# Neighbourhood attention: the block exchange done once per pair of heads

## The chip, the cores and the metric

One Trainium2 chip; the kernel runs on one of its cores. The metric is device time in microseconds (us). The engines are TensorE (PE in the profile, its weight loads PEld), VectorE (DVE), ScalarE (ACT), GpSimd (POOL) and the sync engine (SP), which here only issues DMA transfers. Each engine works through its own queue in order.

## What is computed

One step of a two-layer trunk: 512 latent tokens on an 8 x 64 grid and 128 prompt tokens, 1024 wide, 16 heads of 64. Layer 0 mixes tokens by 2-D neighbourhood attention, layer 1 by grouped-query attention; a gated ConvFFN follows each. The change touches only the attention of layer 0:

```python
s_lat = einsum('brqhd,brkwhd->bhrqkw', qg, kg) * scale        # latent keys: 8 rows x 64 columns
s_lat = where(col_ok, s_lat + bias, -inf)                      # 16 columns around the query's
s_ctx = einsum('brqhd,bchd->bhrqc', qg, k_ctx) * scale         # 128 cached context keys
p = softmax(concatenate([s_lat, s_ctx]))
o = p_lat @ v_lat + p_ctx @ v_ctx                              # then o @ w_o: the output projection
```

Everything is float32. The large products are made of three products of a high and a low part each (`passes`, `wsplit`).

## The kernel before

**One head.** `Head(h)` has four score tiles (slots 0 to 3, 128 queries each). `scores(slot)` issues two products on TensorE into a PSUM bank, the addition of the bias table and the minimum on VectorE, the exponential on ScalarE, a reciprocal on VectorE, the scaling on GpSimd and a transpose on VectorE, which works within blocks of 32 x 32. What it leaves in `p` must still be moved between the partitions, 32 at a time: `exchange` does that with 16 transfers on the sync queue from `p` to `px`. The transfer for target group k and source group q takes 32 partitions and reads all four slots, so the first of them must wait for the last slot.

**A pair of heads.** `values(two)` multiplies the exchanged blocks of an even head and the odd one behind it with the value tiles, 24 products into one bank (`po`), reading `px` through `block`. ScalarE then copies the result to an output tile `of` (one for each pair, 128 x 640). Pairs 0 to 3 are stored to DRAM (`of_store`) and read back later (`ofr`), pairs 4 to 7 stay. `o_split(p)` makes the high and low parts `oh` and `ol` that the output projection reads; `m0.part0(t, p)` is one part of that projection, three products of 512 columns for token tile t and pair p (`y` in the profile).

**The order of the work.** A helper binds all instructions of TensorE to the order in which they are written. The other engines' instructions are ordered by the framework's scheduler at build time, those that it finds ready first, mostly in the order of the program. The loop over the heads follows lists of steps. While head h is in the loop, `s0` to `s3` are the score tiles of head h + 1, `x` its exchange, `f` one part of other TensorE work (`fill`), `a` a part of the modulation row (`ada`), `p0` to `p2` prompt attention (only where h % 4 is 1), `v` the values of heads h - 1 and h. `ORDER0` is for h = 0, `ORDER[0]` for even and `ORDER[1]` for odd heads below 13, `ORDER2` for those from 13 on. A last `f` of a list is left out where h % 4 is 0 and h > 0.

Up to head 12 the work behind `f` is the projection to queries, keys and values (`qk`, `vp`: 6 or 9 products), 173 parts in all, and then four parts of the output projection. What is left after head 12 is worked off, and 26 further parts of the output projection (pairs 2 to 5 for two token tiles, pairs 0 to 5 for the other three) are then spread by `f` over the last heads. Behind the loop stand part 6 for all five token tiles, the split of output tile 7, and part 7.

**Buffers.** `p` and `px` have two buffers of one head (6 KB per partition each), `of` four, the bias table `tb` two, the raw weights `wr` four slots. All weight loads stand in the same sync queue as the exchange and the stores.

Of the kernel before, what the change touches and what calls it, by code (L numbers as in the profile page):

```python
# [10 lines left out]
F32 = mybir.dt.float32  # L11
# [8 lines left out]
P = 128  # L20
# [5 lines left out]
NT = T // P  # L26
# [11 lines left out]
GAP = T + 2  # L38
QW = T + 64
NPT = 2  # L40
NPX = 2
NOF = 4
QD = 32
NAR = 2
OW = {0: 0, 2: 1, 4: 2}
# [3 lines left out]
NC = 3  # L49
QKH = (slice(0, 256), slice(256, T))  # L50
CTX = 2
ORDER0 = "f s0 f f s1 f f s2 f f a f s3 f f f x f f f".split()
ORDER = (
    "f s0 f f s1 f f s2 f f a f s3 f f f x f f f".split(),
    "p0 f s0 f f s1 f p1 f f s2 f f v a p2 s3 f f x".split(),
)
ORDER2 = (
    "f s0 f f s1 f f s2 f f f s3 f f f x f f f".split(),
    "p0 f s0 f f s1 f p1 f f s2 f f v p2 s3 f f x".split(),
)  # L60
PRO = 20
PSTEP = (4, 6, 6, 7, 8, 9)
# [12 lines left out]
def raw_ap(ap, offset, dims):  # L75
    return bass.AP(tensor=ap.tensor, offset=ap.offset + offset, ap=[list(d) for d in dims])
# [30 lines left out]
def hybrid_step(ctx: ExitStack, tc: tile.TileContext, A, O):  # L107
    nc = tc.nc
# [9 lines left out]
    def mm(*a, **k):  # L118
        pe(nc.tensor.matmul(*a, **k))  # L119

    def turn(*a, **k):
        pe(nc.tensor.transpose(*a, **k))  # L122
# [7 lines left out]
    def pool(name, bufs=1, side="left", **k):  # L130
        return tc.tile_pool(name=name, bufs=bufs, side=side, reuse_waits="tile", **k)

    cst = ctx.enter_context(pool("cst"))
    wp = ctx.enter_context(pool("wp", 4))
# [79 lines left out]
    class Halves:  # L214
# [5 lines left out]
        def __init__(self, keep, tmp):  # L220
            self.B = {n: [keep.tile([P, 4, TH], F32R, name=f"B{n}{i}") for i in range(2)] for n in ("11", "21")}
            self.h = tmp.tile([P, KC, 2 * TH], F32, name="hF")
            for c0, c1 in ((NS, NS + 1), (GAP - 1, 2 * TH)):
                nc.gpsimd.memset(self.h[:, :, c0:c1], 0.0)

        def block(self, i, j, c0=0, c1=TH):
            return self.h[:, 4 * i : 4 * i + 4, TH * j + c0 : TH * j + c1]
# [106 lines left out]
    def drain(gen):  # L334
        for _ in gen:
            pass
# [140 lines left out]
    def of_tile(p):  # L477

        if p not in of0:
            of0[p] = opool.tile([P, T], F32, tag="of", name=f"of{p}", bufs=NOF)  # L480
        return of0[p]
# [229 lines left out]
    def prompt_turn(ap, pp, tag, nb):  # L711
        tp = bk.get("tp")
        for i in range(4):
            turn(tp[:, i * P : i * P + P], pp[:, i, :], ident)
        x = ap.tile([P, 512], F32, tag=tag, name="ptp", bufs=nb)
        nc.scalar.copy(x, tp)
        bk.put(tp)
        return x.rearrange("p (a b) -> p a b", a=4)
# [68 lines left out]
    with l_na:  # L787
        ap = l_na.enter_context(pool("na", 2))
# [144 lines left out]
        def na_table(h):  # L933
            if h not in runs:
                na_runs(h)
            tr = runs.pop(h)
            tb = tbs[h % 2]
            for w, dst in ((1, tb[:, 0::6, :]), (0, tb[:, 1:3, :]), (0, tb[:, 4:6, :])):
                t0 = tr[:, w, :]
                rv = raw_ap(t0, RUN - 1, [t0.ap[0], [-16, 2], [-1, 16], [-31, 8]])  # L940
                i = nc.gpsimd.tensor_sub(
                    dst.rearrange("p c (a b) -> p c a b", b=8),
                    mask[:, w].rearrange("p (c a) b -> p c a b", c=2), rv,
                )
                if h == 2:
                    behind(i, plast[0])
            return tb

        class Head:


# [5 lines left out]

            def __init__(self, h):
                self.h, self.b = h, h % 2
                self.p4 = ap.tile([P, 4, 4, 3, QD], F32, tag="p", name="p", bufs=NPT)  # L960
                self.tb = na_table(h)
                self.nm = sm.tile([P, 4], F32, name="nm")
                self.su = sm.tile([P, 4], F32, name="su")
                self.rc = sm.tile([P, 4], F32, name="rc")
# [23 lines left out]

            def exchange(self):

                self.px = ap.tile([P, 4, 4, 3, QD], F32, tag="px", name="px", bufs=NPX)
                for q in range(4):
                    for k in range(4):
                        nc.sync.dma_start(self.px[QD * k : QD * k + QD, q], self.p4[QD * q : QD * q + QD, k])

            def block(self, s0, s1):

                c0 = 3 * QD * s0[0] + QD * s0[1]
                c1 = 3 * QD * s1[0] + QD * s1[1]
                return raw_ap(self.px, c0, [self.px.ap[0], [c1 - c0, 2], [12 * QD, 4], [1, QD]])  # L1000

        def values(two):

# [17 lines left out]
        m0 = Mix(0, A["na_w_o"][0], lambda p, t: tuple(x[:, t * P : t * P + P] for x in osp0[p]))  # L1021
# [44 lines left out]
        work = stream()  # L1066
# [5 lines left out]
        def fill(n=1):  # L1072
            for _ in range(n):
                next(work, None)
# [3 lines left out]
        head = Head(0)  # L1078
        for slot in range(4):
            head.scores(slot)  # L1080
            fill(slot < 3)
        head.exchange()
        for h in range(H):
            nxt = Head(h + 1) if h + 1 < H else None
            g = h // 4
            pr = h % 4 == 1
            order = (ORDER if h < 13 else ORDER2)[h % 2] if h else ORDER0
            for i, step in enumerate(order):
                if step == "f":
                    if i < len(order) - 1 or h % 4 or not h:  # L1090
                        fill()
                elif step == "a":
                    next(ada0, None)
                elif step[0] == "s" and nxt:
                    nxt.scores(int(step[1]))
                elif step == "x" and nxt:
                    nxt.exchange()
                elif step == "v":
                    values((before, head))
                if pr and step == "p0":  # L1100
                    sides = []
                    for hh in range(4 * g, 4 * g + 4):
                        qs, kh, kl = qk_of[hh // 2]
                        b = hh % 2
                        sides.append((qs[b][:, QW - P :], kh[b][:, T:], kl[b][:, T:]))
                    pp = prompt_scores(ap, sides)
                if pr and step == "p1":
                    pth = prompt_turn(ap, pp, "ptp", 1)
                if pr and step == "p2":
                    po = bk.get("po")  # L1110
                    for j in range(2):
                        for b in range(2):
                            mm(po[64 * b : 64 * b + 64, j * P : j * P + P], vts_of[g][:, 4, 2 * j + b, :],
                               pth[:, 2 * j + b, :], start=True, stop=True)
                    for j in range(2):
                        nc.scalar.copy(of_tile(2 * g + j)[:, NS:T], po[:, j * P : j * P + P])
                    bk.put(po)
            if h % 2 and h < 8:
                of_store(h // 2)
            before = head  # L1120
            head = nxt
            if h == 11:
                def early(ps, *rows_):
                    for ts in rows_:
                        for p in ps:
                            for t in ts:
                                m0.part0(t, p)
                                yield

                work = chain(work, early(range(OEARLY), range(2)))  # L1130
                drain(ada0)
                l_ada.close()
                epool = l_na.enter_context(pool("o0e", 1))
                osp0.extend([epool.tile([P, T], F32R, name=f"o{i}{p}") for i in "hl"] for p in range(OEARLY))
                for p in range(OEARLY):
                    o_split(p)
            if h == 12:
                drain(work)
                r_h0.close()
                hpool = r_na.enter_context(pool("o0h", 1, "right"))  # L1140
                osp0.extend([hpool.tile([P, T], F32R, name=f"o{i}{p}") for i in "hl"] for p in range(OEARLY, KC))
                for p in range(OEARLY, 4):
                    o_split(p)
                m0.weights(0, 3)
                for p in range(4, 6):
                    o_split(p)

                work = chain(early(range(OEARLY, 6), range(2)), early(range(6), range(2, NT)))
            if h == 13:
                o_split(6)  # L1150
        drain(work)
        for t in range(NT):
            m0.part0(t, 6)
        o_split(7)
    hp1 = ExitStack()
    xmp = ExitStack()
# [359 lines left out]
    ap = gqs.enter_context(pool("gp", 2, "right"))  # L1516
# [290 lines left out]
    for hq in range(2):  # L1807
        for n, t in enumerate(((4, 0, 1, 2, 3), (0, 1, 2, 3, 4))[hq]):
# [4 lines left out]
            if i in (8, 9):  # L1813
                for k in range(4):
                    ada_raws.append(wp.tile([P, D], F32, tag=("wh", "wl")[k % 2], name="wa"))
                    k = len(ada_raws) - 1
                    nc.sync.dma_start(ada_raws[k], A["ada_w"][1, k * P : k * P + P, 3 * D : 4 * D])
            if n == 2:
                a, b = gqa_prompt(2 * hq), gqa_prompt(2 * hq + 1)
# [10 lines left out]
    with ExitStack() as s:  # L1830
        ap = s.enter_context(pool("ga", 2, "right"))
# [147 lines left out]
```

## Time and profile before

| | us |
|---|---|
| median of 3 runs (lowest, highest) | 1595.76 (1592.12, 1595.95) |
| profiled execution, own time | 1591.86 |
| its span, first to last instruction | 1590.1 |
| TensorE busy in the span | 1510.3 |
| VectorE, ScalarE, GpSimd busy | 1036.0, 845.3, 700.0 |
| the 256 exchange transfers issued | from 78.9 to 357.9 |

Rows of the timeline read: start, length, engine, line, operation, output <- inputs, shape, count, and in brackets the idle time of the engine before the row and what ended it. Rows of a group read: count, then busy time and mean of one in ns, then idle time ahead of the group and what ended it. `SPq` rows are issues of transfers, not the transfers. Line 119 is the helper of all matmuls, so its rows are told apart by their tiles.

### The profile page before, as it was taken

How to read it: one execution, taken by the hardware profiler on the slowest of the kernel's cores; microseconds unless marked ns; L12 is line 12 of the kernel's file. 1: busy time of each engine (PE TensorE's matmuls, PEld its weight loads, DVE VectorE, ACT ScalarE, POOL GpSimd, SP SyncE). 2: the span in 40 equal slices, each digit the busy share in tenths (PEclk: the TensorE clock that was granted, in tenths of full speed). 3: DMA queues.
4: the chain of work that ended last, by engine and by line, in shares of the span. 5: the costliest groups of instructions: out<-in, count | busy, mean ns of one | idle time of the engine just before them, and what ended most of it. 6: DMA issues, size and time to landing. Idle time of an engine off the chain costs nothing.

```text
span 1590.1 us, 26190 instructions
## 1 busy us (share of the span) xinstructions
PE 1510.3 (95%) x9549; PEld 1338.5 (84%) x9549; DVE 1036.0 (65%) x1680; ACT 845.3 (53%) x1608; POOL 700.0 (44%) x606
## 2 busy tenths in 40 slices
PE   6987888879999999999999999999999999999998
PEld 5976778757999999988887887878899999998886
DVE  4543444446976766775475778774788888776554
ACT  5554545525665555554454446764656656554443
POOL 1544454413145455543454455441325655553433
PEclk9999999989999999999999999999999999999999
DMA  9756665447276566348666412003733434448664
GB/s 324 189 163 155 170 172 146 128 129 239 88 230 214 184 220 189 119 169 286 219 225 226 109 65 83 15 1 114 238 121 94 124 105 145 131 159 267 212 219 136
DMA packets 210109, 259.22 MB, mean 163 GB/s; under 512 B 15708, under 2 KB 165436, under 8 KB 209980
## 3 DMA queue, kind: packets, MB, share of 16 engines
q1 hardware_dynamic: 200144, 250.97, 49.8%
q10 hardware_dynamic: 9836, 6.59, 2.1%
q8 instruction: 75, 1.23, 0.3%
q14 instruction: 54, 0.44, 0.1%
HBM read 215.69 MB, written 27.65 MB: 153 GB/s over the span
## 4 chain that ended last, share of the span: by engine, by line
PE 62%; DVE 6%; ACT 2%; issue 2%; POOL 1%; DMA 1%; POOLq 0%; DVEq 0%; ACTq 0%; SPq 0%
PE acc L119 18%; PE ux L119 16%; PE uz L119 8%; PE gp L119 5%; PE uy L119 4%; PE po L119 2%; PE y L119 2%; PE s L119 2%; PE tp L122 2%; PE ada L119 1%; DMA wr<-in_ffn_w_up 1%; DVE t L1298 1%; ACT gp L1709 1%; DVE al L1221 0%; ACT t L1296 0%
## 5 line engine op out<-in xcount | busy, mean ns | idle before, releaser
L182 POOL TENSOR_TENSOR wl<-wr,wh 128x1024 fp32r<-128x1024 f32 x70 | 172.2, 2464 | 240.2 <-ACT wh L180 239.7
L1221 POOL TENSOR_TENSOR wl<-wr,wh 128x1024 fp32r<-128x1024 f32 x76 | 183.4, 2435 | 47.3 <-ACT wh L1220 43.7
L119 PE MATMUL ux<-B,wh 128*128 128x322 f32 x832 | 200.1, 311 | 1.0 <-ACT u L1275 0.9
L1298 DVE SCALAR_TENSOR_TENSOR t<-C,cw,t 128x644 f32<-128x644 f32 x176 | 156.2, 888 | 50.2 <-ACT t L1296 49.6
L119 PE MATMUL acc<-wh,alo 128*128 128x512 f32 x440 | 172.3, 392 | 0.3 <-DVE alo L1190 0.3
L180 ACT CAST wh<-wr 128x1024 fp32r<-128x1024 f32 x140 | 145.6, 1048 | 49.9 <-DMA wr<-in_ffn_w_down 33.4
L119 PE MATMUL acc<-wh,ahi 128*128 128x512 f32 x440 | 171.9, 391 | 0.0
L119 PE MATMUL acc<-wl,ahi 128*128 128x512 f32 x440 | 171.8, 391 | 0.0
L119 PE MATMUL uz<-B,wh 128*128 128x322 f32 x640 | 156.2, 312 | 1.4 <-ACT v L1275 1.4
L119 PEld LDWEIGHTS ux<-B,wh 128*128 128x128 f32 x832 | 143.6, 189 | 3.7 <-ACT u L1275 2.0
L1190 DVE TENSOR_TENSOR alo<-ain,ahi 128x384 fp32r<-128x384 f32 (+1 forms) x88 | 81.8, 948 | 87.6 <-ACT ahi L1188 87.2
L119 PE MATMUL ux<-B,wl 128*128 128x322 f32 x416 | 129.5, 311 | 3.3 <-DVE wl L1221 3.3
L119 PE MATMUL qk<-hT,wh 128*128 128x384 f32 (+1 forms) x512 | 124.8, 318 | 0.0
L119 PEld LDWEIGHTS uz<-B,wh 128*128 128x128 f32 x640 | 110.9, 189 | 4.8 <-ACT v L1275 2.0
L1221 POOL TENSOR_TENSOR vl<-wr,vh 128x1024 fp32r<-128x1024 f32 x38 | 96.4, 2536 | 24.7 <-ACT vh L1220 24.3
L1220 ACT CAST wh<-wr 128x1024 fp32r<-128x1024 f32 x84 | 84.8, 1049 | 39.8 <-DVE wr L1244 39.4
L182 DVE TENSOR_TENSOR wl<-wr,wh 128x1024 fp32r<-128x1024 f32 x70 | 91.3, 1315 | 22.0 <-ACT wh L180 21.4
L1296 ACT ACTIVATE t<-C,cw 128x644 f32<-128x644 f32 x88 | 78.6, 893 | 47.9 <-DVE C L1326 41.0
L119 PE MATMUL uz<-B,wl 128*128 128x322 f32 x320 | 99.6, 311 | 0.4 <-POOL wl L1221 0.3
L119 PEld LDWEIGHTS acc<-wh,alo 128*128 128x128 f32 x440 | 82.6, 188 | 18.8 <-DVE alo L1190 1.1
L119 PEld LDWEIGHTS acc<-wl,ahi 128*128 128x128 f32 x440 | 82.6, 188 | 17.9
L119 PEld LDWEIGHTS acc<-wh,ahi 128*128 128x128 f32 x440 | 82.6, 188 | 17.7
(258 smaller groups left out, 3839.7 us busy)
## 6 DMA issues: line engine op xcount, KB each, us to landing
wr<-in_ffn_w_up SPq DMA_DIRECT2D x88, 512.0 KB
wr<-in_ffn_w_down SPq DMA_DIRECT2D x88, 512.0 KB
wr<-in_ada_w SPq DMA_DIRECT2D x72, 512.0 KB
act<-act SPq DMA_DIRECT2D x44, 321.0 KB
wr<-in_na_w_qkv SPq DMA_DIRECT2D x24, 512.0 KB
px<-p SPq DMA_DIRECT2D x256, 48.0 KB
mod<-modrow SPq DMA_DIRECT2D x20, 512.0 KB
ain<-act SPq DMA_DIRECT2D x44, 192.0 KB
```

The source lines that it names most:

```text
L119: pe(nc.tensor.matmul(*a, **k))
L122: pe(nc.tensor.transpose(*a, **k))
L180: i = nc.scalar.copy(hi, raw)
L182: j = (low or nc.vector).tensor_sub(lo, raw, f32(hi))
L1190: pin(nc.vector.tensor_sub(lo[:, 0 : c1 - c0], ain[:, 0 : c1 - c0], f32(hi[:, 0 : c1 - c0])))
L1220: nc.scalar.copy(hl[0], src)
L1221: low.tensor_sub(hl[1], src, f32(hl[0]))
L1296: nc.scalar.activation(t, taps(0), AF.Identity, bias=cw[:, 3, n : n + 1], scale=cw[:, 1, n : n + 1])
L1298: nc.vector.scalar_tensor_tensor(t, taps(d), cw[:, w, n : n + 1], t, op0=ALU.mult, op1=ALU.add)
L1709: nc.scalar.activation(self.pt[i].rearrange("p (a b) -> p a b", a=2), sv, AF.Exp, bias=nm, scale=-1.0, accum_out=su)
```

## The change

`p` and `px` become tiles of a pair, 12 KB per partition: two buffers of `p`, one of `px`. The even head creates the pair's `p`; the odd head writes into its other half. `exchange` is called once for two heads, behind the odd head's last score tile, and its 16 transfers each carry both heads (96 KB where it was 48). `block` addresses the head within the pair. The exchange of head 0 alone, ahead of the loop, goes.

The lists are rewritten: the odd lists hold all four score tiles of the next even head ahead of `v` and have no `x`; the even lists begin with the score tiles of the odd head, and have `x` behind them and the rest of the `f` behind that. From head 13 on the odd head's score tiles follow each other with one `f` or none between, and all remaining `f` stand behind `x`. In addition, for h = 14 the rest of the work and part 6 of the output projection are issued ahead of the loop's last round, which holds the values of heads 14 and 15.

To make room, `of` has two buffers instead of four, so pairs 4 and 5 are also stored and read back, and the prompt's turned probabilities take a slot of `wr` instead of a tile of their own.

```diff
-NPX = 2
-NOF = 4
+NPX = 1
+NOF = 2
-ORDER0 = "f s0 f f s1 f f s2 f f a f s3 f f f x f f f".split()
+ORDER0 = "s0 f s1 f f s2 f f s3 f f x f f a f f f f f".split()
 ORDER = (
-    "f s0 f f s1 f f s2 f f a f s3 f f f x f f f".split(),
-    "p0 f s0 f f s1 f p1 f f s2 f f v a p2 s3 f f x".split(),
+    "s0 f s1 f f s2 f f s3 f f x f f a f f f f f".split(),
+    "p0 f f s0 f f p1 s1 f f s2 f f s3 f v a p2 f".split(),
 )
 ORDER2 = (
-    "f s0 f f s1 f f s2 f f f s3 f f f x f f f".split(),
-    "p0 f s0 f f s1 f p1 f f s2 f f v p2 s3 f f x".split(),
+    ("s0 s1 f s2 f s3 f f x" + 16 * " f").split(),
+    "p0 s0 f s1 f f p1 s2 f s3 f v p2 f".split(),
 )
...
-                self.p4 = ap.tile([P, 4, 4, 3, QD], F32, tag="p", name="p", bufs=NPT)
+                if not self.b:
+                    pair[:] = [ap.tile([P, 4, 2, 4, 3, QD], F32, tag="p", name="p", bufs=NPT)]
+                self.pair = pair[0]
+                self.p4 = self.pair[:, :, self.b]
...
-                self.px = ap.tile([P, 4, 4, 3, QD], F32, tag="px", name="px", bufs=NPX)
+                px[:] = [ap.tile([P, 4, 2, 4, 3, QD], F32, tag="px", name="px", bufs=NPX)]
                 for q in range(4):
                     for k in range(4):
-                        nc.sync.dma_start(self.px[QD * k : QD * k + QD, q], self.p4[QD * q : QD * q + QD, k])
+                        nc.sync.dma_start(px[0][QD * k : QD * k + QD, q], self.pair[QD * q : QD * q + QD, k])
...
-        head.exchange()
         for h in range(H):
...
-                    pth = prompt_turn(ap, pp, "ptp", 1)
+                    pth = prompt_turn(wp, pp, "wr", None)
...
-            if h % 2 and h < 8:
+            if h % 2 and h < 12:
                 of_store(h // 2)
...
-        drain(work)
-        for t in range(NT):
-            m0.part0(t, 6)
+            if h == 14:
+                drain(work)
+                for t in range(NT):
+                    m0.part0(t, 6)
         o_split(7)
```

More of the change, by code (lines that the diff above doesn't have):

```diff
@@ L947, in na_table @@
             return tb
+        pair, px = [None], [None]
         class Head:
@@ L989, in exchange @@
             def exchange(self):
-                self.px = ap.tile([P, 4, 4, 3, QD], F32, tag="px", name="px", bufs=NPX)
+                px[:] = [ap.tile([P, 4, 2, 4, 3, QD], F32, tag="px", name="px", bufs=NPX)]
                 for q in range(4):
                     for k in range(4):
-                        nc.sync.dma_start(self.px[QD * k : QD * k + QD, q], self.p4[QD * q : QD * q + QD, k])
+                        nc.sync.dma_start(px[0][QD * k : QD * k + QD, q], self.pair[QD * q : QD * q + QD, k])
             def block(self, s0, s1):
-                c0 = 3 * QD * s0[0] + QD * s0[1]
-                c1 = 3 * QD * s1[0] + QD * s1[1]
-                return raw_ap(self.px, c0, [self.px.ap[0], [c1 - c0, 2], [12 * QD, 4], [1, QD]])
+                c0 = 12 * QD * self.b + 3 * QD * s0[0] + QD * s0[1]
+                d = 3 * QD * (s1[0] - s0[0]) + QD * (s1[1] - s0[1])
+                return raw_ap(px[0], c0, [px[0].ap[0], [d, 2], [24 * QD, 4], [1, QD]])
         def values(two):
```

## The prediction

> **What bounds the kernel now.** I read the page first, then one window over the attention stage of layer 0, then the groups of instructions by shape in it, then TensorE's and the sync queue's timelines there. The page says that TensorE is the bound nearly everywhere; the window says where it is not.
>
> ```profile
> span 1590.1 us, 26190 instructions
> PE 1510.3 (95%) x9549; PEld 1338.5 (84%) x9549; DVE 1036.0 (65%) x1680; ACT 845.3 (53%) x1608; POOL 700.0 (44%) x606
> 88.00:365.00 277.00, 233.88 (x1611) 203.79 (x1610) 118.74 (x330) 128.11 (x353) 111.56 (x119) 0.93 0.57 156
> L119 PE MATMUL po<-px,vt 128*64 128x256 f32 x192 | 35.1, 482 | 34.4 <-DMA px<-p 32.4 <-issue 2.1
> ```
>
> TensorE idles 1590.1 - 1510.3 = 79.8 us in all, and 277.0 - 233.9 = 43.1 of them lie between 88 and 365 us, where the granted clock is 0.93 (last columns: clock, DMA share, GB/s). No other engine is over half busy there. The last row names the reader that waits: the value products `po`, once per pair of heads, 34.4 us. The eight waits for the exchange, and how long the 22 products behind each took:
>
> ```profile
> 107.93 2.78 PE L119 MATMUL po<-px,vt 128*64 128x256 f32 x22 [0.96 <-DMA px<-p]
> 147.57 4.57 PE L119 MATMUL po<-px,vt 128*64 128x256 f32 x22 [8.14 <-DMA px<-p]
> 185.74 4.27 PE L119 MATMUL po<-px,vt 128*64 128x256 f32 x22 [2.93 <-DMA px<-p]
> 222.76 4.46 PE L119 MATMUL po<-px,vt 128*64 128x256 f32 x22 [4.05 <-DMA px<-p]
> 260.77 2.78 PE L119 MATMUL po<-px,vt 128*64 128x256 f32 x22 [1.94 <-DMA px<-p]
> 294.69 4.40 PE L119 MATMUL po<-px,vt 128*64 128x256 f32 x22 [2.42 <-DMA px<-p]
> 349.88 0.62 PE L119 MATMUL po<-px,vt 128*64 128x256 f32 x2 [2.33 <-DMA px<-p]
> 360.10 4.13 PE L119 MATMUL po<-px,vt 128*64 128x256 f32 x22 [9.60 <-DMA px<-p]
> ```
>
> They sum to 32.4. Twice 22 products take 2.78 us, five times 4.13 to 4.57: after the longer waits the array runs at a lower clock. That adds 1.79 + 1.49 + 1.68 + 1.62 + 1.35 = 7.9 us. So the exchange costs 34.4 + 7.9 = **42.3 us** now.
>
> What is late in it? Pair 3 (heads 6, 7), with the last score tile of head 6, of head 7, the first value product, and the sync queue's issues:
>
> ```profile
> 191.52 0.45 PE L119 MATMUL s<-kh,qs 128*128 128x384 f32 x1
> 204.19 0.33 PE L119 MATMUL s<-kh,qs 128*128 128x384 f32 x1
> 218.06 0.65 PE L119 MATMUL po<-px,vt 128*64 128x256 f32 x2
> 209.19 11.73 SPq L994 DMA_DIRECT2D px<-p  x16
> 240.17 0.35 PE L119 MATMUL s<-kh,qs 128*128 128x384 f32 x1
> 246.28 13.04 SPq L994 DMA_DIRECT2D px<-p  x16
> 277.74 0.33 PE L119 MATMUL s<-kh,qs 128*128 128x384 f32 x1
> 282.21 11.02 SPq L994 DMA_DIRECT2D px<-p  x16
> 310.84 0.34 PE L119 MATMUL s<-kh,qs 128*128 128x384 f32 x1
> 318.54 10.02 SPq L994 DMA_DIRECT2D px<-p  x16
> 341.57 0.34 PE L119 MATMUL s<-kh,qs 128*128 128x384 f32 x1
> 338.25 20.21 SPq L994 DMA_DIRECT2D px<-p  x32
> ```
>
> Head 7's last score tile starts at 204.19; its chain over VectorE, ScalarE and GpSimd lets the exchange begin at 209.19 (5.0 later); the sync queue takes 11.73 to issue 16 transfers (0.73 each), and the products go on 1.84 after the last issue. From last score to data: 18.6 us; for pairs 4 and 5 (240.17 to 260.77, 277.74 to 294.69) 20.6 and 17.0. Mean **18.7**. TensorE's own work from 204.19 to the products ends at 218.7: the need is longer than the cover. In the last pair 32 transfers stand in one row, 20.21 us: head 14's exchange is still being issued when head 15 is ready. The issue, not the mathematics, is the long part.
>
> **The change part by part.** First, the exchange once per pair: 128 issues instead of 256, each of 96 KB instead of 48. What does one cost?
>
> ```profile
> L994 SPq DMA_DIRECT2D px<-p x256: 507/588/1545, 78.9 to 357.9; - x128
> px<-p SPq DMA_DIRECT2D x256, 48.0 KB
> wr<-in_ada_w SPq DMA_DIRECT2D x72, 512.0 KB
> 227.85 0.82 SPq L295 DMA_DIRECT2D wr<-in_ada_w  x2
> 115.82 14.69 SPq L994 DMA_DIRECT2D px<-p  x16
> 340.00:360.00 20.00, 8.16 (x36) 6.13 (x34) 2.89 (x9) 1.34 (x4) 1.61 (x5) 0.82 0.33 80
> ```
>
> A 512 KB load is issued in 0.41 us and a 48 KB exchange in 0.59 (median): size does not set it. I take 10.0 to 14.7 us for 16, as now, 11.5 in the middle. Bounds: unchanged below, twice that above, if the time went with bytes. The transfers themselves: from 340 to 360 us hardly anything but the exchange moved, 80 GB/s x 20 us = 1.6 MB, and the engines were 0.33 busy: 6.6 us for a pair's bytes, under 11.5. So a pair's need stays 18.7 us from the odd head's last score, and the even head's 16 issues, some 8 x 11.5 = 92 us of the sync queue, vanish.
>
> Second, the order, which sets the cover. One work step `f`: from 191.52 to 218.06 stand 24 `f`, 8 score tiles (0.35 each) and one modulation part (1.0): (26.54 - 2.8 - 1.0)/24 = 0.95 us. Before, 6 + 8 `f` lie between the odd head's last score and the values. After, it is 2 + 7 behind it in the even list and 9 in the odd one: 18 `f`, five score tiles, one part = 17.1 + 1.75 + 1.0 = **19.8 us** (one `f` less in two pairs, whose prompt products take its place). Against needs of 18.6, 20.6 and 17.0 that leaves 0, 0.8 and 0. Pairs 0 to 5: 3 us in all; below 0, above 20 (each as bad as 3 us over, the 14.69 case).
>
> Third, pair 6. Behind head 13's last score come 8 `f` (three or four of the short kind below), 4 score tiles, the prompt products and 5 short `f`: 0.35 + 6.2 + 1.4 + 1.4 + 3.5 = 12.9 us, less than now, plus what TensorE waits there anyhow; its need was at most 18.6 (310.84 to 329.4, no wait then). A stall of 4 us; bounds 0 and 12. The upper end is a queue effect: output tiles 4 and 5 now go to DRAM and back (`h < 12`, NOF 2), two stores and two loads more on the sync queue, about 0.5 us each:
>
> ```profile
> 315.23 1.00 SPq L1027 DMA_DIRECT2D ofr<-of0d  x2
> 341.92 0.39 PE L119 MATMUL y<-wh,oh 128*128 128x512 f32 x1
> 342.62 0.40 PE L119 MATMUL y<-wh,oh 128*128 128x512 f32 x1
> 364.26 1.09 ACT L1016 COPY of<-po 128x384 f32<-128x384 f32 x3 [20.54 <-PE po L119]
> 365.38 0.73 ACT L1030 CAST oh<-of 128x640 fp32r<-128x640 f32 x1
> 366.14 0.82 DVE L1031 TENSOR_TENSOR ol<-of,oh 128x640 fp32r<-128x640 f32 x1 [20.93 <-ACT oh L1030]
> ```
>
> Now both loads went ahead of head 13's exchange (315.23 against 318.54). If the two new ones land behind a 16-transfer block, the projection part of tile 4 waits some 10 us for them.
>
> Fourth, pair 7. A projection `f` is three products: 342.62 - 341.92 = 0.70 us. Behind head 15's last score come 18 of them and the five of part 6: 23 x 0.70 + 0.35 = 16.4 us. Its need, with the sync queue free: four tiles within 2.8 us crowd VectorE (ready some 6.5 us after the last, an estimate from the 5.0 of pair 3), then 10.1 (half of 20.21), then 1.6: 18.2. Stall 2; bounds 0 and 8. But part 6 now stands ahead of the values, so the split of output tile 7 has lost its cover: copies 1.09, cast 0.73 (oh at +1.9 after the products), low part to +2.8, while two products of 0.23 can start. That is 2.3 us idle, and 1.5 for the clock.
>
> Here a rule is weighed. The trace lowers the clock after 2.42 us of waiting and not after 1.94. The Trainium skill, "TensorE: Matmul & The Clock Gate", Part 1, puts the fall after an idle window of about 3.4 us; this trace is stricter. By the page the 1.5 would be 0 and the sum 1.5 us better.
>
> Fifth, score tiles stand closer, while the three smaller engines work in order:
>
> ```profile
> 87.39 0.66 PE L119 MATMUL s<-kh,qs 128*128 128x384 f32 x1 [5.63 <-DVE qs L892]
> PE tp L122 <- POOL pp L708: 4.0, 2, 2.2
> ```
>
> Such waits (5.6 at 87, 4.0 for the prompt turns) stay; I add 3 us, bounds -3 and +10 (each doubled). At nothing: the wider strides of `p` and `px` (the same elements), one `px` buffer (it is rewritten some 8 `f` after its last reader), two `of` buffers, and the prompt's turned tile in a slot of `wr`, held for about 10 us: it is covered by the three other slots, and the load behind it has 14 `f`, 13 us, until its user; without that cover it costs up to 10 us once per four heads, in the +10 above.
>
> Sum: 42.3 - 3 - 4 - 2 - 3.8 - 3 = **26.5 us less**. The profiled execution took 1591.86 (span 1590.1 and 1.76 around it) and becomes 1565.4. It was as fast as the quickest of the three runs; their median, 1595.76, is 3.9 higher. I predict 1568, between 1565.4 and 1569.3.
>
> **The rivals.** (a) Transfers bound the pair. If 96 KB takes longer per transfer, the need grows by 16 times that. Gains and losses meet where each pair has 3.3 us more, a pitch of 0.93 us against 0.72. At 1.08, half way to doubling, each pair stalls 6 us more: 48 less 26.5 plus about 8 for the clock = 30 us slower, 1625. For it: the 14.69 us block (0.92 each) beside loads. Against: 6.6 us of engine time, and products that go on 1.5 to 1.8 us after the last issue. The Trainium skill, "DMA: Bandwidth & Descriptors", section "Issuing engines are not separate DMA queues", holds that issue time is usually small beside the DMA itself, which would point this way; the rows here have it the other way round. (b) The loads of tiles 4 and 5 stand behind pair 6's block: 10 us lost, 1578. (c) The crowded scores hold TensorE at their banks: VectorE waits for GpSimd in order, so the 5.63 us wait appears in two or three more heads: about 14 us, 1582. (d) The cover was not what failed: the exchange simply starts later, since other issues stand ahead of it, and the time stays, 1593. Against: the need of pairs 3 to 5 is made up of the chain and 16 issues alone.
>
> **How the numbers follow.** Forecast 0.58, (a) 0.09, (b) 0.13, (c) 0.13, (d) 0.07. The forecast's own range from the bounds is 1554 to 1580. With (b), (c) and most of (d) the range is 1552 to 1592. A measurement of this kernel tells 0.3% (5 us) from no change; faster by more: 0.58 + 0.13 + 0.13 = 0.84; within: (d), 0.07; slower: (a), 0.09.
>
> **What would show it.** Right: the `po` group's idle falls from 34.4 to under 12; 128 issues of `px` with a median near 0.6 us, blocks of 10 to 13 us; the granted clock between 88 and 340 over 0.96; a gap of about 2 us between the last `po` and the first part-7 product. Wrong: blocks of 15 us and more (a); waits of `y` for `ol` near the middle of the projection (b); waits of `s` or `qk` for VectorE (c).

## The result, and the profile after

The changed kernel takes 1575.72 us (median of 4 runs, 1574.36 to 1577.02), the kernel before beside it 1594.97 (4 runs, 1592.12 to 1595.95): ratio 0.9882, 95% interval 0.9865 to 0.9899, so 19.25 us less, where 1568 (some 27 less) was forecast. The profiled execution was its slowest, 1577.02 with a span of 1575.0; that of before, 1591.86, was quicker than all four. The profiled pair therefore differs by 14.8 only, and stages are compared below by their own rows.

Two lines of the page of the changed kernel, then three other views in the order of the prediction:

```profile
span 1575.0 us, 25917 instructions
PE 1507.6 (96%) x9549; PEld 1335.4 (85%) x9549; DVE 1037.2 (66%) x1680; ACT 843.3 (54%) x1608; POOL 710.2 (45%) x606
```

The window (the last three columns are clock, DMA share and GB/s):

```profile
88.00:365.00 277.00, 243.62 (x1663) 210.08 (x1662) 127.84 (x343) 139.06 (x380) 120.76 (x130) 0.97 0.67 184
```

The group and the tile:

```profile
L119 PE MATMUL po<-px,vt 128*64 128x256 f32 x176 | 24.6, 436 | 6.7 <-DMA tr<-in_k_rpb 3.7 <-ACT qs L891 1.6 <-DMA px<-p 1.2
L999 SPq DMA_DIRECT2D px<-p x128: 507/591/2225, 90.7 to 341.8; - x128
```

In the same 277 us TensorE is busy 243.62 in place of 233.88 us, at a clock of 0.97 in place of 0.93. The value products idle 6.7 us (34.4 before). The view puts only 1.2 of that down to the exchange and 3.7 to a load of bias rows (`tr`), which these products do not read. By the rows below, all four of their waits are the exchange's: the products of pairs 1, 3, 5 and 7 start 1.9 to 2.1 us behind the last issue of their own block, which ends at 141.71, 209.41, 280.05 and 342.36. An issue still takes 0.59 us at twice the bytes. What TensorE waits for now stands in the view of its waits, from 78 to 345 us; these are its first four lines (total, times, longest):

```profile
PE vp L119 <- POOL wl L182: 6.9, 6, 2.5
PE y L119 <- ACT oh L1035: 3.9, 1, 3.9
PE po L119 <- DMA tr<-in_k_rpb: 3.7, 1, 3.7
PE tk L122 <- ACT kp L906: 3.3, 1, 3.3
```

The first line is new: the products of V's weights (`vp`) wait for the low part `wl` of those weights. The second is rival (b) in small. TensorE's and the sync queue's timelines show both, and the values of pairs 1, 3, 5, 6 and 7 with their waits:

```profile
118.72 0.53 PE L119 MATMUL vp<-wl,hT 128*128 128x256 f32 x1 [2.50 <-POOL wl L182]
143.78 2.81 PE L119 MATMUL po<-px,vt 128*64 128x256 f32 x24 [1.21 <-DMA px<-p]
211.46 2.81 PE L119 MATMUL po<-px,vt 128*64 128x256 f32 x24 [1.59 <-ACT qs L891]
281.99 4.50 PE L119 MATMUL po<-px,vt 128*64 128x256 f32 x24 [3.67 <-DMA tr<-in_k_rpb]
303.43 10.10 SPq L999 DMA_DIRECT2D px<-p  x16
313.63 1.02 SPq L1032 DMA_DIRECT2D ofr<-of0d  x2
317.56 0.80 PE L119 MATMUL y<-wh,oh 128*128 128x512 f32 x1 [3.87 <-ACT oh L1035]
319.15 4.99 PE L119 MATMUL po<-px,vt 128*64 128x256 f32 x24
344.25 2.81 PE L119 MATMUL po<-px,vt 128*64 128x256 f32 x24 [0.23 <-issue]
348.92 0.50 PE L119 MATMUL y<-wh,oh 128*128 128x512 f32 x1 [1.86 <-ACT oh L1035]
```

The two loads of spilled rows stand right behind pair 6's 16 issues. The product that needs them waits 3.87 us, and the values behind it run at a lower clock (4.99 against 2.81).

### The profile page after: what moved, and what is told of

Its sections match the earlier page's. It is cut to its first block, busy times and chain, and to the rows that moved or that the text cites. A ratio compares the mean times of both kernels' runs of the same rounds, so it can differ in the third digit from the quotient of the medians.

```text
span 1575.0 us, 25917 instructions
## 1 busy us (share of the span) xinstructions
PE 1507.6 (96%) x9549; PEld 1335.4 (85%) x9549; DVE 1037.2 (66%) x1680; ACT 843.3 (54%) x1608; POOL 710.2 (45%) x606
## 4 chain that ended last, share of the span: by engine, by line
PE 63%; DVE 5%; ACT 2%; issue 2%; POOL 1%; DMA 1%; ACTq 0%; POOLq 0%; DVEq 0%; SPq 0%
PE acc L119 18%; PE ux L119 17%; PE uz L119 8%; PE gp L119 5%; PE uy L119 4%; PE po L119 2%; PE y L119 2%; PE s L119 2%; PE tp L122 2%; PE ada L119 1%; DMA wr<-in_ffn_w_up 1%; DVE t L1303 1%; ACT gp L1714 1%; ACT t L1301 0%; DVE wl L182 0%
## 5 line engine op out<-in xcount | busy, mean ns | idle before, releaser
L1226 POOL TENSOR_TENSOR vl<-wr,vh 128x1024 fp32r<-128x1024 f32 x38 | 106.2, 2794 | 26.2 <-ACT vh L1225 25.9
L119 PEld LDWEIGHTS acc<-wh,alo 128*128 128x128 f32 x440 | 82.6, 188 | 18.9 <-DVE alo L1195 1.2
```

Source lines behind the costliest of these rows:

```text
L1226: low.tensor_sub(hl[1], src, f32(hl[0]))
```

## Experiments

Theory A, from the prediction: the cover was too short, the issue of 16 transfers is the long part of the need, and halving the issues and moving the work behind the exchange both pay. The rivals differ from run to run. The ratio is to the kernel before in the same call (medians 1593.1 to 1594.9).

| run | what it is | us | ratio [95%] |
|---|---|---|---|
| order_alone | before, new lists | 1596.34 | 1.0013 [0.9996, 1.0031] |
| merge_alone | changed, old lists | 1594.57 | 1.0003 [0.9989, 1.0016] |
| issues_32 | changed, each transfer cut in two | 1627.96 | 1.0217 [1.0197, 1.0238] |
| loads_on_act | changed, two loads on ScalarE's queue | 1571.03 | 0.986 [0.984, 0.988] |
| turn_in_pp | changed, no slot of `wr` lent | 1561.04 | 0.9806 [0.9783, 0.9828] |
| part6_behind | changed, part 6 behind the values | 1578.87 | 0.9908 [0.9887, 0.9929] |
| two_queues | changed, half of the issues on ScalarE's queue | 1595.28 | 1.0013 [0.9997, 1.0029] |
| merge_no_loan | merge_alone, no slot of `wr` lent | 1593.12 | 0.9996 [0.9983, 1.0009] |
| loan_alone | before, a slot of `wr` lent | 1612.6 | 1.0108 [1.0087, 1.0128] |
| both_edits | loads_on_act and turn_in_pp together | 1558.74 | 0.9776 [0.9755, 0.9796] |

**Lists alone.** The kernel before, with all lists and part 6's place as in the changed kernel, except that the odd lists keep an `x` behind `v`; tiles of one head, 256 issues. One of the lists:

```diff
-ORDER0 = "f s0 f f s1 f f s2 f f a f s3 f f f x f f f".split()
+ORDER0 = "s0 f s1 f f s2 f f s3 f f x f f a f f f f f".split()
...
```

> The kernel before with the new lists of steps alone (and part 6 ahead of the last values): tiles of one head, 256 transfers of 48 KB, the even head's exchange right behind the values of the pair ahead. Theory A (what was missing is cover between the odd head's last score tile and its values): the even head's block is out of the way some 15 us after the values, the odd head's follows, so pairs 0 to 5 wait about 1 us each and the last pair about 6; idle of the value products 10 to 16 us, time near 1581. Theory B (the halved number of issues is what pays): the waits stay near 30 us and the time near 1592.

It took 1596.34 us, no gain. The idle time at the values did fall, to 8.3 us, below what Theory A expected, but the time is nearer Theory B's, since other readers wait in its stead:

```profile
L119 PE MATMUL po<-px,vt 128*64 128x256 f32 x186 | 27.4, 412 | 8.3 <-DMA px<-p 7.1 <-issue 1.2
```

Its waits of TensorE, from 78 us:

```profile
PE y L119 <- ACT oh L1030: 13.0, 2, 11.2
PE qk L119 <- DVE qs L892: 7.8, 3, 3.2
PE ada L119 <- DMA wr<-in_ada_w: 7.6, 7, 2.3
```

And its sync queue at the block of pair 6:

```profile
315.95 10.02 SPq L994 DMA_DIRECT2D px<-p  x16
326.02 1.05 SPq L1027 DMA_DIRECT2D ofr<-of0d  x2
```

The cover is there, but with 32 issues for each pair the sync queue is still full, and the loads behind a block come late: one wait of 11.2 us is for the rows loaded at 326.02, behind the block of 315.95.

**Halved issues alone.** The changed kernel with all lists as before (without the `x` of the odd ones) and part 6 behind the values. One of the lists:

```diff
-    "p0 f f s0 f f p1 s1 f f s2 f f s3 f v a p2 f".split(),
+    "p0 f s0 f f s1 f p1 f f s2 f f v a p2 s3 f f".split(),
...
```

> The changed kernel with the old lists of steps, the odd lists without x: 128 transfers of 96 KB, but only 14 f between the odd head's last score tile and its values, and part 6 behind the values. Theory A: each of pairs 0 to 5 needs 18.6 to 20.6 us against a cover of 13.9, so it waits 5 to 6 us, the last pair about 7; idle of the value products 30 to 37 us, time 1590 to 1596, no gain. Theory B: idle under 20 us, time near 1580.

1594.57 us, no gain either, as Theory A had it. The values still idle 26.6 us (it said 30 to 37), 18.9 of it for the exchange, and V's products wait 13.8 at a bank that VectorE empties:

```profile
L119 PE MATMUL po<-px,vt 128*64 128x256 f32 x178 | 31.1, 517 | 26.6 <-DMA px<-p 18.9 <-DVE p L992 3.0 <-ACT qs L891 2.4
```

The line of V's products in the view of waits:

```profile
PE vp L119 <- DVE kl L864: 13.8, 3, 4.9
```

Fewer issues hardly bring the odd head's data sooner, since the need runs from its last score tile: in pairs 1 to 5 it is 16.5 to 18.8 us from there to the products, where it was 16.9 to 22.7 before.

**Twice the issues at the same bytes.**

```diff
-nc.sync.dma_start(px[0][QD * k : QD * k + QD, q], self.pair[QD * q : QD * q + QD, k])
+for b in range(2):
+    nc.sync.dma_start(px[0][QD * k : QD * k + QD, q, b], self.pair[QD * q : QD * q + QD, k, b])
```

> The changed kernel, but each of its 16 transfers cut into one per head: 32 issues of 48 KB in one block, the same bytes. If the issue sets the block (as the prediction took it): blocks of 20 to 23 us instead of 10 to 14, each pair some 9 us later, idle of the value products 70 us or more, time near 1650. If the bytes or the transfers set it: blocks stay at 10 to 14 us and the time near 1576.

1627.96 us: the direction of Theory A, short of its size, and in another place. Only the block of the last pair is a clean comparison. Its 32 issues follow each other without a pause and take 20.66 us, where the 16 of the changed kernel take 10.04: with the same bytes the block doubles, so issue sets it. The blocks of the first five pairs, 25.64 to 31.69 us, hold pauses as well: a transfer of one head no longer needs both heads, so the block starts early and then stops until the odd head's `p` is ready (6.9 us of nothing issued in the row at 196.56). TensorE pays at readers of loads behind the block, more than at `po` (10.9 us idle):

```profile
196.56 31.69 SPq L1000 DMA_DIRECT2D px<-p  x32
372.96 20.66 SPq L1000 DMA_DIRECT2D px<-p  x32
```

TensorE's waits in it:

```profile
PE qk L119 <- ACT wh L180: 15.0, 2, 13.9
PE y L119 <- ACT oh L1036: 9.8, 1, 9.8
```

**The loads of output tiles 4 and 5.**

```diff
-nc.sync.dma_start(x, of0d[p])
+(nc.scalar if p in (4, 5) else nc.sync).dma_start(x, of0d[p])
```

> The changed kernel with one edit: the two spilled rows that output tiles 4 and 5 read back are issued on ScalarE's queue and no longer on the sync queue, where their 1.02 us of issue stood directly behind the 10.10 us block of pair 6 (start 303.43, loads at 313.63). Theory A (the wait of 3.87 us of the first output product on the cast of these rows is the sync queue's block, and the lower clock of the values product behind it, 4.99 us in place of 2.81, follows from that wait): the loads go out at about 304, the wait of 3.87 goes to under 1, the values product of pair 6 takes 2.8, sum 5 to 6 us less than the changed kernel's 1575.7, so about 1570. Rival B (the load waits for its own buffer or for the store of these rows, not for the queue): wait stays at 3 to 4 us, time 1575 to 1577. Rival C (ScalarE is late itself, with two issues more in front of its exponentials): the wait goes to the scores of head 14 or 15, time 1575 to 1578.

1571.03 us, 4.7 less than the changed kernel by the medians; the intervals of the two ratios overlap a little. The trace is clearer:

```profile
304.09 0.33 ACTq L1032 DMA_DIRECT2D ofr<-of0d  x1
312.33 0.66 PE L122 MATMUL tp<-ident,pp 128*128 128x128 f32 x4 [3.49 <-POOL pp L708]
315.01 2.81 PE L119 MATMUL po<-px,vt 128*64 128x256 f32 x24
```

The loads go out at 304, the wait of 3.87 us is gone, and pair 6's values take 2.81. Part of the gain goes to a prompt turn ahead of them that now waits 3.49.

**The lent slot.** The changed kernel puts the prompt's turned probabilities into a slot of the weight rows' pool `wr`. Here they share the buffer of the prompt's probabilities.

```diff
-pth = prompt_turn(wp, pp, "wr", None)
+pth = prompt_turn(ap, pp, "pp", 1)
```

> The changed kernel with one edit: the prompt's turned probabilities lie in the buffer tag of the prompt's probabilities (one buffer) and no longer in a slot of the weight-row pool, so that a weight load never has to wait for that slot. Theory A (the waits of V's product on GpSimd's split of the weight rows, 6.9 us in 6 waits, come from a weight load that stands behind the slot lent to the prompt): these go to under 1.5 us, with the clock behind them about 4 to 6 us less than the changed kernel's 1575.7, so 1570 to 1572. Rival B (GpSimd has too much in its own row at these places: the prompt's scores, the split and the additions): they stay at 5 to 7 us, time 1575 to 1577. A cost that either may meet: the turned probabilities now wait until the prompt's probabilities of the next group have been read, or the next group's probabilities wait for the turned ones to be used, which would show as TensorE waits on the prompt's probabilities of more than the 1.8 us of the changed kernel.

1561.04 us, 14.7 less than the changed kernel by the medians (12 by the ratios) and more than Theory A expected. Its sync queue and GpSimd, ahead of V's products for the second group, and its values of pairs 1 and 6:

```profile
60.13 24.51 SPq L176 DMA_DIRECT2D wr<-in_na_w_qkv  x6
90.18 12.53 SPq L999 DMA_DIRECT2D px<-p  x16
91.30 2.37 POOL L182 TENSOR_TENSOR wl<-wr,wh 128x1024 fp32r<-128x1024 f32 x1 [0.74 <-POOL tb L941]
99.80 2.40 POOL L182 TENSOR_TENSOR wl<-wr,wh 128x1024 fp32r<-128x1024 f32 x1 [0.24 <-ACT wh L180]
138.23 2.81 PE L119 MATMUL po<-px,vt 128*64 128x256 f32 x24 [0.59 <-ACT p L984]
301.82 0.79 PE L119 MATMUL y<-wh,oh 128*128 128x512 f32 x1 [3.84 <-ACT oh L1035]
303.40 5.13 PE L119 MATMUL po<-px,vt 128*64 128x256 f32 x24
```

The same stretch in the changed kernel:

```profile
60.20 0.39 SPq L176 DMA_DIRECT2D wr<-in_na_w_qkv  x1
90.75 12.83 SPq L999 DMA_DIRECT2D px<-p  x16
104.79 0.94 SPq L176 DMA_DIRECT2D wr<-in_na_w_qkv  x2
112.10 2.38 POOL L182 TENSOR_TENSOR wl<-wr,wh 128x1024 fp32r<-128x1024 f32 x1 [3.75 <-ACT wh L180]
116.32 2.34 POOL L182 TENSOR_TENSOR wl<-wr,wh 128x1024 fp32r<-128x1024 f32 x1
```

TensorE's instructions stand in the same order in both kernels; the sync queue's do not. With the slot lent, the two loads of V's weights stand behind the exchange block: issued at 104.79, split at 112.10 and 116.32, and V's product waits at 118.72. Without the loan they go out ahead of it, and the splits are done at 102. The waits of `vp` for `wl` (6.9 us) are gone, and those of pairs 1, 3 and 5 with their lower clock fall from 1.21 + 1.59 + 3.67 + 1.69 (4.50 less 2.81) = 8.2 to 0.6. These two add up to 6.9 + 7.6 = 14.5, beside 14.7 by the medians; but the other waits moved both ways (`qk` for VectorE 7.9 where it had 1.7), so the close agreement is partly chance. The record of the queue shows where the loads went; why the scheduler put them there is not in a trace.

**Part 6 behind the values again.**

```diff
             if h == 14:
                 drain(work)
-                for t in range(NT):
-                    m0.part0(t, 6)
+        for t in range(NT):
+            m0.part0(t, 6)
```

> The changed kernel with one edit: output projection part 6 stands behind the values of the last pair again, as in the kernel before, and no longer ahead of them; the tail of the last pair then has only what is left of the list as cover. Theory A (part 6 is the cover of the last pair: without its 12 products, between 300 and 600 ns each in the part's rows, the wait of the last pair's values grows from 0.23 by 4 to 6 us, and the gap of 1.86 us ahead of the first product of part 7 goes, since part 6 fills it): net 2 to 4 us more than the changed kernel, 1578 to 1580. Rival B (the two cancel, because the copies of output tile 7 that part 7 waits for take as long as the exchange still lacks): 1575 to 1577. Rival C (the gap was the dearer of the two, with a clock lowered behind it): 1572 to 1575.

1578.87 us, 3.2 more than the changed kernel, inside overlapping intervals. The last pair waits 3.65 in place of 0.23 and loses 1.7 by the clock, and the gap of 1.86 us ahead of part 7 is gone:

```profile
341.69 4.50 PE L119 MATMUL po<-px,vt 128*64 128x256 f32 x24 [3.65 <-DMA px<-p]
```

By these rows 3.65 - 0.23 + 1.69 - 1.86 = 3.3 more, as Theory A had it. The times do not show it: the intervals overlap, and the two profiled executions differ by 0.7 us only (1577.75 and 1577.02); other rows moved too, as pair 5's products, 2.81 here and 4.50 in the changed kernel. That part 6's new place is worth about 3 us is read from the rows alone.

**Two queues.**

```diff
-nc.sync.dma_start(px[0][QD * k : QD * k + QD, q], self.pair[QD * q : QD * q + QD, k])
+(nc.sync, nc.scalar)[k % 2].dma_start(px[0][QD * k : QD * k + QD, q], self.pair[QD * q : QD * q + QD, k])
```

> The changed kernel with one edit: of the 16 transfers of a pair, 8 are issued on the sync queue and 8 on ScalarE's queue, alternately. Theory A (issue sets the block: 10.0 to 13.8 us for 16 issues in one queue): each queue's 8 issues take 5 to 7 us, the values' data land 4 to 6 us earlier, and the values' waits on data and the wait on the spilled rows behind pair 6 (3.87) go to under 1 us; if ScalarE's 5 us for each of 8 pairs found it free, the time would be 5 to 8 us less, about 1568 to 1571. Theory A with a price (ScalarE's issues wait for the probabilities of the odd head, and the exponentials and evictions behind them on ScalarE stand for the chain of 5 to 9 us from score to probability and for 5 us of issue): the scores behind wait for ScalarE, 2 to 6 us for each of 8 pairs, the time 1575 to 1610, and this is the likelier of the two. Rival B (transfers, not issue, set the block): the blocks together stay at 10 to 13 us and the data land as late as before.

1595.28 us; the whole gain is lost, as the version with a price expected. Eight issues take 6.2 to 7.6 us in each queue, where 16 in one took 10.0 to 13.8, so the transfers do not set the block and Rival B is out. No value product waits for data, but ScalarE's own work stands behind its issues:

```profile
139.91 6.95 ACTq L999 DMA_DIRECT2D px<-p  x8
146.90 0.93 ACT L501 COPY vt<-vp 128x256 f32<-128x256 f32 x3 [6.65 <-DMA px<-p]
```

TensorE waits for that engine (view of waits):

```profile
PE sp L119 <- ACT kh L863: 16.5, 7, 5.2
PE tk L122 <- ACT kp L906: 13.2, 2, 7.8
```

**The loan in the other kernels.** Two runs ask what the lent slot costs by itself, and whether it hid the worth of the halved issues in merge_alone. Both use the line of turn_in_pp, one way or the other.

> The run with the halved exchange and the old lists (merge_alone, 1594.57 us), with one edit more: the prompt's turned probabilities lie in the buffer of the prompt's probabilities and take no slot of the weight-row pool. Theory A (the lent slot costs about 15 us wherever the work steps lie, and so hid what the halved exchange is worth by itself): 1594.6 less 15 is 1580, between 1577 and 1584, and the values' idle time stays at 20 us or more, since the old lists give the last transfer too little cover. Rival B (the lent slot hurts only with the new lists, in which the score tiles stand close and the prompt's products come late): 1591 to 1597. Rival C (with the slot back, the halved exchange is the whole of the gain, and the lists are worth nothing): 1560 to 1566.

1593.12 us, 1.5 less than merge_alone by the medians: Rival B. V's products no longer wait 13.8 us, but the value products wait 37.8 us in all, 36.3 of it for the exchange, where they waited 26.6: what is not waited for at the one is waited for at the other.

```profile
PE po L119 <- DMA px<-p: 36.3, 7, 10.0
```

> The kernel before with one edit of the change alone: the prompt's turned probabilities take a slot of the weight-row pool; lists, 256 issues and the order of the projection parts are as before. Theory A (the lent slot by itself costs the 14.7 us by which the changed kernel gained when it was taken back): 1595 plus 12 to 18, so 1607 to 1613, with V's product waiting on GpSimd's split. Rival B (before, the sync queue is so full with 256 exchange issues that a load which waits for a slot waits beside them, and the idle time at the values takes it in): 1595 to 1600.

1612.6 us, 18.6 more than before, about as Theory A had it. But it had V's products waiting on the split, and they do not; the values wait longer for the exchange. The view of TensorE's waits has, from 78 us to the end of the stage:

```profile
PE po L119 <- DMA px<-p: 46.2, 8, 9.5
```

Before, the same line had 32.4. In pairs 2 to 5 it is now 21.0 to 23.3 us from the odd head's last score tile to the products, where it was 16.9 to 20.6. So the loan costs 15 to 19 us by the medians (12 to 17 by the ratios) in two of the kernels and next to nothing in the third. Why the old lists with 256 issues feel it and those with 128 do not is not settled by these runs.

**Both edits that helped.**

> The changed kernel with the two edits that helped: the prompt's turned probabilities in the buffer of the prompt's probabilities (1561.0 us alone), and the loads of the spilled rows of output tiles 4 and 5 on ScalarE's queue (1571.0 alone, 4.7 less than the changed kernel). Theory A (the two waits are separate: that of the first output product on the cast of the spilled rows, 3.84 us in the run with the first edit alone, with 5.13 us for the values behind it in place of 2.81, goes on top): 1561.0 less 4 to 6 is 1555 to 1557. Rival B (the row's wait falls only to its next limit, the cast on ScalarE, and the time goes to the scores behind): 1559 to 1562.

1558.74 us, 2.3 less than turn_in_pp by the medians, between A and B; the intervals overlap, so the second edit's gain on top is not shown by the times. The row that it was meant for did clear: pair 6's values take 2.81 where they took 5.13, and again a prompt turn ahead waits 3.49.

```profile
301.97 2.81 PE L119 MATMUL po<-px,vt 128*64 128x256 f32 x24
```

At 0.9776 [0.9755, 0.9796] of the kernel before, this is the quickest version here, ahead of the changed kernel.

## Why the prediction was right, and where it was off

The direction and the mechanism held, and the time lies in the forecast's own range. That it came within 8 us of the forecast is partly luck: one term put at nothing cost more than that, and others were too dear. The signs that it named came: idle time at the values 6.7 (said under 12), 128 issues of 0.59 us, blocks of 10.0 to 13.8 us (10 to 13), clock 0.97 (over 0.96), a gap of 1.86 ahead of part 7 (about 2).

- **Recovered time, 42.3.** Right. Without the loan the values wait 0.9 us in all, and every pair but pair 6 runs its products in 2.81.
- **Issue, not bytes (rival a).** Right: 0.59 us at 96 KB as at 48, and in the last pair 20.66 us for 32 issues in place of 10.04 for 16. The Trainium skill, "DMA: Bandwidth & Descriptors", "Issuing engines are not separate DMA queues", has issue time as usually small beside the transfer; for a row of 16 of these transfers inside the chip the runs disagree, with 10.0 us and more of issue and the reader 1.9 to 2.1 us behind the last.
- **One queue's blocks and the cover, taken as two gains.** The prediction let the even head's 92 us of sync queue vanish and put no price on it. The runs show that, without the loan, neither part pays alone (1596.34, 1593.12) and that together they pay 32 us (1561.04 against 1593.13): the lists make the cover, and the halved issues let the loads behind the block through.
- **The lent slot, costed at nothing. This is the step that failed.** The prediction took it as held for about 10 us, covered by three other slots and 14 `f`, with a possible 10 us in a bound. It was held that long (copied at 100.4, read until 109.7), but its cost is not the hold: with the slot lent, the loads of V's weights stand behind the next exchange block in the sync queue. It measured 14.7 us by the medians, more than the whole miss of about 8: without it the change gains 32 us, so the rest of the sum was some 5 us too cautious.
- **Pairs 0 to 5, 3 us.** Measured 8.2, of which 7.6 went with the loan. Without the loan 0.6 is left, so the term was large enough, though not by its parts. Pair 1 needs 20.7 us in the changed kernel (last score tile of the odd head at 123.06, data at 143.78) in place of 18.7, since its block starts 5.8 us behind that score and takes 12.9; in pairs 2 to 6 it starts 7.0 to 9.3 behind. The prediction took 5.0 from the kernel before.
- **Pair 6, 4 us.** Measured 3.87 + 2.18 (4.99 less 2.81) = 6.1: rival (b), with a wait where it said the products of tile 4 would wait, but 3.87 and not 10 us: TensorE had other work until 313.7. loads_on_act shows the cause.
- **Pair 7 and the split, 2 and 3.8 us.** Measured 0.23 and 1.86. The clock did not fall behind 1.86 us of waiting; 1.5 of the 3.8 was for that.
- **Crowded scores, 3 us.** Without the loan, TensorE's other waits from 78 to 345 us are some 17 against 14 before: right in size. Rival (c) did not come in the changed kernel, where `qk` waits 1.7 us for VectorE. Without the loan its sign does show, small: `qk` waits 7.9 us for VectorE in three heads, where before one score tile waited 5.6.

Almost 3 us of what the stage gained went again behind it: the first part-7 product starts 18.8 us earlier than before (367.69 to 348.92), the first up-projection product 18.1 (401.4 to 383.3), the last accumulations of that layer 16.0. Why was not tried.

## What to carry to other kernels

Price a borrowed buffer by what it does to the order of the queue behind it, not by how long it is held: list the loads that draw on the pool, and see which of them would then stand behind a long block of issues. Where one queue carries both an exchange and the loads, neither more cover nor fewer issues need pay alone; try them together before giving either up. When waits fall at the reader that you aimed at but the time stands still, read the same queue's other passengers next.

## What the runs showed of the hardware that was not expected

Bytes do not set the issue of such a transfer, and the length of a block is not its issues alone. In the last pair, where little else moves, 16 of 96 KB take 10.04 us and 32 of 48 KB 20.66 (0.63 and 0.65 each):

```profile
332.32 10.04 SPq L999 DMA_DIRECT2D px<-p  x16
```

In the middle of the stage 16 take up to 13.81. There, too, most issues follow each other at 0.63 us; what lengthens the block is a few long issues (up to 2.2 us) and pauses in which nothing is issued (2.45 us from 93.93 in the changed kernel). In the trace each issue behind such a pause waits for the semaphore that it will raise itself, and an earlier transfer, often a load, was the last to use that semaphore: so it waits for that transfer to land. In the kernel before, the view of the sync queue's own waits has, next to the wait for `p`:

```profile
SPq L994 <- DMA wr<-in_ada_w: 10.7, 8, 3.4
SPq L994 <- DMA tr<-in_k_rpb: 8.2, 7, 2.8
```

These are loads of weights and of bias rows, from which the exchange takes nothing. So a block also lengthens when loads are still under way beside it; no run varies that by itself.

Split over two queues, eight issues take 6.2 to 7.6 us in each (0.78 to 0.95 each): two queues do not halve the block.

The lower clock does not follow from the length of the wait alone. In the changed kernel it came behind 3.67 us (24 products in 4.50, 2.81 otherwise) and not behind 1.59 and 1.86; the kernel before had it behind 2.42. But merge_alone has it behind 1.91, with a granted clock of 0.63 in those products, and part6_behind runs at full speed behind 2.89:

```profile
104.70 4.50 PE L119 MATMUL po<-px,vt 128*64 128x256 f32 x24 [1.91 <-DMA px<-p]
278.93 2.81 PE L119 MATMUL po<-px,vt 128*64 128x256 f32 x24 [2.89 <-DMA tr<-in_k_rpb]
```

So the limit between 1.94 and 2.42 us that the prediction read from the kernel before does not hold in the other runs. The Trainium skill, "TensorE: Matmul & The Clock Gate", Part 1, gives an idle window of about 3.4 us; the runs have the fall behind waits as short as 1.91.
